# Spreading norm factors as two float32r parts, and state-space products of two heads in turn, in a hybrid decoder layer

## The chip, the cores and the metric

The kernel runs on one core of one Trainium2 chip. The metric is the device time of one execution in microseconds (us); a stated time is the median of several runs. Profiles are of one execution. The engines are named as in the profile: PE is the matrix engine (TensorE), PEld its weight loads, DVE VectorE, ACT ScalarE, POOL GpSimd and SP SyncE, which here only starts transfers.

## What is computed

One layer on 512 tokens of 1024 features, all in float32. Shortened from the reference:

```python
h = x
h = h + 0.5 * swiglu(rmsnorm(h, ffn1_norm), ...)               # D_FF 2816
n = rmsnorm(h, mix_norm)
u, v, z, xbc, dt_raw = split(n @ w_in)                         # 1024, 1024, 1024, 1536, 16
ya = rmsnorm(chunked_spatial_gating(gelu(u), gelu(v)), gm_out_norm)
yb = mamba2_mixer(z, xbc, dt_raw, ...)                         # ends in an rmsnorm in two groups
h = h + concatenate([ya, yb]) @ w_out
h = h + 0.5 * swiglu(rmsnorm(h, ffn2_norm), ...)
gate = sigmoid(rmsnorm(h, ple_norm) @ ple_w_gate + ple_b_gate)
h = h + gate * (p @ ple_w_proj)
return rmsnorm(h, final_norm)
```

An rmsnorm multiplies every token by one factor, rsqrt of the mean of its squared features (plus a small constant), and every feature by a gain. Inside the Mamba-2 mixer (`ssd_chunked`) the 512 tokens are cut into four chunks of 128, and 16 heads of 64 features share two groups of B and C vectors with 128 state features. Per head and chunk, with C·B a 128x128 matrix of the group:

```python
y_diag = ((C B) * decay_of_the_head) @ (x * dt)                # inside the chunk
y_off  = (C @ state_carried_into_the_chunk) * exp(a_cs)        # chunks 1, 2, 3 only
y      = y_diag + y_off + x * d_skip
y      = y * silu(z)                                           # then the rmsnorm of the group
```

## The kernel before, in words

**Layout.** Everything is kept with features on the 128 partitions and the 512 tokens along the free axis, so one tile is 128 features by 512 tokens, and 1024 features are eight tiles. Chunk c of a tile is its columns 128c to 128c+127.

**Large products.** A float32 weight or activation is cut in two float32r numbers, a high part (a copy rounded to float32r) and a low part (the number less its high part). A product is made of three float32r passes, high with high, high with low, low with high (`passes`, lines 199 to 201, called by `accumulate`). The FFNs use the same three passes on sums and differences of tiles (line 617). Weights come by DMA; ACT makes the high part (line 417), DVE the low part (line 421).

**Order of the work.** The whole kernel but its last stage is a list of steps, each a product with its load and split. `run` writes the instruction order of PE, ACT, DVE and SP from that list: the product of a step, the split of the weights for a later step, what was put "after" a step, and what was put on PE behind the product of a step. These engines then execute in exactly that order; only the last stage (per-layer embedding and final norm) is ordered by the scheduler. The mix stage's steps have the order "B0 B1 dt C0 C1 x0 v0 x1 x2 x3 v1 x4 x5 v2 x6 x7 z0 v3 z1 v4 z2 v5 z3 v6 z4 v7 z5 u0 z6 u1 z7 u2 ... u7", each a projection of 128 features (B, C, x, z, u feature-major, v token-major). `first(n, ...)` and `post(n, ...)` put work of DVE, ACT and POOL at step n, ahead of and behind its other work; `on_pe(n, ...)` puts PE work behind the product of step n.

**A norm** (`Norm`, from line 234). Squares are summed over the tiles; PE sums them over the partitions with a column of ones (`sums`), which gives one number per token with tokens on the partitions, 128x4. `of_sums` takes the rsqrt there in small DVE steps (lines 214 to 222). To multiply feature-major tiles, the factor of each token is needed on all 128 partitions. `diagonals` (DVE, line 280) multiplies an identity matrix by the factors, four 128x128 diagonal matrices side by side in one 128x512 tile of the ring "tmp", which has three buffers. `spread` (PE, line 291) multiplies them by a 128x128 matrix of ones in float32: every output row is then the row of factors. `kept` (ACT, line 297) copies that from PSUM to SBUF, the tile "rall". Seven norms go this way: ahead of the first FFN, ahead of the mix stage, the two groups of the Mamba-2 mixer, the spatial gating's output (in the code "gm"), ahead of the second FFN, and ahead of the per-layer embedding.

In the first FFN the first factors meet the gate at line 721 (DVE), after `kept`. DVE writes a tile "embt" (line 528) behind the first diagonal, and ACT copies it to "xfa" (line 530) ahead of `kept`.

**State-space products.** The heads are taken in eight pairs j = 0 to 7; pairs 0 to 3 are of group 0. For a pair, one step of the list after another: ACT turns two tiles of cumulated sums into decays (`decayed`, lines 1313 and 1317); DVE multiplies each head's decays by C·B (`times_cb`, line 1321); PE does `ssd`; DVE and POOL add and gate the result (`gated`, from line 1342); its square is added to the norm of its group. `ssd(j)` stands on PE behind the product of the step after z_j. Its products are float32. For y_diag (line 1331) there are eight: for head 0 and then head 1, for each of the four chunks, one product with 64 columns of x·dt as weights (64 features) and the head's 128x128 decays as moving data. Head 0's results go to partitions 0 to 63 of the PSUM bank `pa`, head 1's to partitions 64 to 127. For y_off (line 1336) there are three, for chunks 1 to 3, each with the carried state of both heads, all 128 features, as weights and the chunk's C as moving data, into the bank `pb`.

Group 0's norm follows pair 3, group 1's pair 7 (`normed_group`): sums on PE behind one product, diagonals on DVE at the next step, spread on PE behind that step's product. The spatial gating's `spatial` takes sums of tiles over partitions with float32r ones (line 1422) from the high and low parts "convin" (ACT line 183, DVE line 184).

In the prediction, "pair 1" to "pair 8" are j = 0 to 7.

## Time and profile before

| quantity | value |
|---|---|
| median of 3 runs | 1097.27 us (1097.17 to 1097.84) |
| span of the profiled execution | 1096.2 us |
| PE matmuls | 1079.8 us, 99% of the span, 6639 instructions |
| PE weight loads | 952.6 us, 87% |
| DVE | 777.0 us, 71%, 1057 instructions |
| ACT | 520.4 us, 47%, 715 instructions |
| POOL | 153.6 us, 14%, 139 instructions |
| moved by DMA | 161.67 MB, on average 147 GB/s |
| line 417, high parts of weights, ACT, 138 of the shape 128x1024 | 144.3 us, 1045 ns each |
| line 421, low parts of weights, DVE, 137 of them | 172.8 us, 1261 ns each |

The span is the time between the first and the last instruction of one core's execution. Times of instructions are counted from its start. A row of the timeline has the start, the duration, the engine, the line of the code, the operation, output<-inputs, their sizes, and x with the number of instructions that the row joins; in brackets stands the time that the engine waited ahead of it and what released it. A float32 product leaves two records of PE, a float32r product one, so that the eight products of line 1331 are "x16". A wait is written as engine, tile and line that waits, an arrow, and the engine, tile and line that released it, then the time in all, the number of waits and the longest. A row of the stretches has begin:end, length, then the busy time and number of instructions of PE, PEld, DVE, ACT and POOL, then the granted clock of PE (1.00 is full), the busy share of DMA, and GB/s; where one line of code is selected, an engine that has none of it is left out.

### The profile page before, as it was taken

How to read it: one execution, taken by the hardware profiler on the slowest of the kernel's cores; microseconds unless marked ns; L12 is line 12 of the kernel's file. 1: busy time of each engine (PE TensorE's matmuls, PEld its weight loads, DVE VectorE, ACT ScalarE, POOL GpSimd, SP SyncE). 2: the span in 40 equal slices, each digit the busy share in tenths (PEclk: the TensorE clock that was granted, in tenths of full speed). 3: DMA queues.
4: the chain of work that ended last, by engine and by line, in shares of the span. 5: the costliest groups of instructions: out<-in, count | busy, mean ns of one | idle time of the engine just before them, and what ended most of it. 6: DMA issues, size and time to landing. Idle time of an engine off the chain costs nothing.

```text
span 1096.2 us, 16449 instructions
## 1 busy us (share of the span) xinstructions
PE 1079.8 (99%) x6639; PEld 952.6 (87%) x6639; DVE 777.0 (71%) x1057; ACT 520.4 (47%) x715; POOL 153.6 (14%) x139
## 2 busy tenths in 40 slices
PE   9999999999999999999999999999999999999997
PEld 7789999999998788787878888889999999999886
DVE  7787776776666696756888566678766776767766
ACT  6554434344444455474673343454444344344554
POOL 3411000000000300133223000000000000000411
PEclk9999999999999999999999999999999999999999
DMA  9758766565623233444333233567766766643412
GB/s 358 202 148 235 193 161 177 168 188 149 177 56 117 80 97 95 135 135 135 101 111 96 77 97 106 176 159 213 198 158 183 193 178 188 163 126 101 147 41 78
DMA packets 49037, 161.67 MB, mean 147 GB/s; under 512 B 5568, under 2 KB 5824, under 8 KB 48960
## 3 DMA queue, kind: packets, MB, share of 16 engines
q1 hardware_dynamic: 38288, 124.80, 33.8%
q0 software_dynamic: 9232, 33.56, 16.9%
q10 hardware_dynamic: 1440, 2.26, 0.6%
q8 instruction: 52, 0.85, 0.3%
q14 instruction: 25, 0.20, 0.1%
HBM read 156.33 MB, written 4.26 MB: 146 GB/s over the span
## 4 chain that ended last, share of the span: by engine, by line
PE 87%; DVE 6%; ACT 3%; issue 2%; DMA 1%; SPq 0%; POOL 0%; DVEq 0%; ACTq 0%; POOLq 0%
PE mm L617 18%; PE a L617 14%; PE sm L200 10%; PE sm L199 10%; PE sm L201 10%; PE mm L200 4%; PE mm L201 4%; PE mm L199 4%; PE a L199 3%; PE a L201 3%; PE a L200 3%; DVE wlo L421 2%; ACT whi L417 1%; DMA h<-in_x 1%; PE sm L1331 1%
## 5 line engine op out<-in xcount | busy, mean ns | idle before, releaser
L417 ACT CAST whi<-raw 128x1024 fp32r<-128x1024 f32 x138 | 144.3, 1045 | 167.2 <-issue 58.9
L421 DVE TENSOR_TENSOR wlo<-raw,whi 128x1024 fp32r<-128x1024 f32 x137 | 172.8, 1261 | 66.5 <-ACT whi L417 62.8
L617 PE MATMUL mm<-xfb,whi 128*128 128x256 f32 x960 | 166.7, 276 | 0.2 <-ACT a L731 0.2
L617 PEld LDWEIGHTS mm<-xfb,whi 128*128 128x128 f32 x960 | 146.2, 188 | 2.0 <-ACT a L731 0.4
L617 PE MATMUL mm<-xfb,wlo 128*128 128x256 f32 x480 | 133.0, 277 | 0.3 <-DVE wlo L421 0.3
L201 PE MATMUL sm<-ghi,wlox 128*128 128x512 f32 x296 | 116.3, 393 | 0.0
L200 PE MATMUL sm<-glo,whix 128*128 128x512 f32 x296 | 115.9, 391 | 0.0
L199 PE MATMUL sm<-ghi,whix 128*128 128x512 f32 x296 | 115.1, 389 | 0.0
L617 PE MATMUL a<-xfb,whi 128*128 128x256 f32 x640 | 111.2, 276 | 1.0 <-DVE g L749 1.0
L617 PEld LDWEIGHTS a<-xfb,whi 128*128 128x128 f32 x640 | 97.9, 188 | 3.2 <-issue 1.6
L617 PEld LDWEIGHTS mm<-xfb,wlo 128*128 128x128 f32 x480 | 90.2, 188 | 0.7 <-DVE wlo L421 0.7
L617 PE MATMUL a<-xfb,wlo 128*128 128x256 f32 x320 | 88.6, 277 | 1.1 <-DVE wlo L421 1.1
L421 DVE TENSOR_TENSOR wlox<-rawd,whix 128x1024 fp32r<-128x1024 f32 (+1 forms) x40 | 45.7, 1142 | 59.0 <-ACT whix L417 59.0
L421 DVE TENSOR_TENSOR wlo<-rawb,whi 128x1024 fp32r<-128x1024 f32 x52 | 64.7, 1246 | 25.1 <-ACT whi L417 24.9
L755 ACT ACTIVATE g<-g 128x512 f32<-128x512 f32 x40 | 25.3, 632 | 108.9 <-DVE g L754 108.9
L632 POOL DMA_DIRECT2D raw<-in_ffn_gu x20 | 17.2, 860 | 390.5 <-DVE h L809 108.1
L809 DVE SCALAR_TENSOR_TENSOR h<-sm,h 128x512 f32<-128x512 f32 x96 | 63.2, 684 | 5.9 <-PE sm L201 5.3
L251 POOL TENSOR_TENSOR ssum<-ssum,tmp 128x512 f32<-128x512 f32 x33 | 50.0, 1514 | 123.3 <-ACT tmp L250 117.6
L417 ACT CAST whi<-rawb 128x1024 fp32r<-128x1024 f32 x52 | 54.1, 1043 | 26.7 <-DVE rawb L627 20.0
L201 PEld LDWEIGHTS sm<-ghi,wlox 128*128 128x128 f32 x296 | 55.5, 188 | 11.6
L199 PEld LDWEIGHTS sm<-ghi,whix 128*128 128x128 f32 x296 | 55.6, 188 | 10.9
L200 PEld LDWEIGHTS sm<-glo,whix 128*128 128x128 f32 x296 | 55.5, 188 | 10.8
(410 smaller groups left out, 2537.0 us busy)
## 6 DMA issues: line engine op xcount, KB each, us to landing
raw<-in_ffn_gu SPq DMA_DIRECT2D x56, 512.0 KB, 5.7
rawd<-in_ffn_down SPq DMA_DIRECT2D x40, 512.0 KB, 4.0
rawb<-in_ffn_gu SPq DMA_DIRECT2D x32, 512.0 KB, 5.3
raw<-in_ffn_gu POOLq DMA_DIRECT2D x30, 512.0 KB, 5.5
raw<-in_w_in SPq DMA_DIRECT2D x29, 512.0 KB, 3.6
s<-in_ffn_gu SPq DMA_DIRECT2D x20, 512.0 KB, 7.0
s<-in_ffn_gu POOLq DMA_DIRECT2D x20, 512.0 KB, 8.3
raw<-in_w_out SPq DMA_DIRECT2D x16, 512.0 KB, 3.5
```

The costliest lines, as they stand in the source:

```text
L199: nc.tensor.matmul(ps, whi, xhi, start=first, stop=False)
L200: nc.tensor.matmul(ps, whi, xlo, start=False, stop=False)
L201: nc.tensor.matmul(ps, wlo, xhi, start=False, stop=last)
L251: self.engines[i].tensor_tensor(self.totals[i], self.totals[i], sq, ALU.add)
L417: nc.scalar.copy(self.hi[:, : self.n], self.raw[:, : self.n])
L421: nc.vector.tensor_tensor(self.lo[:, :n], self.raw[:, :n], self.hi[:, :n].bitcast(F32), ALU.subtract)
L617: nc.tensor.matmul(o, wt[:, c], xt, start=fresh and p == m == n == 0, stop=last and n == 2, skip_group_check=True,)
L632: nc.gpsimd.dma_start(w21.raw, self.src[0], accum_op=ALU.add)
L755: nc.scalar.activation(t, t, AF.Silu)
L809: nc.vector.scalar_tensor_tensor(h[d], ps[d], 0.5, h[d], ALU.mult, ALU.add)
L1331: nc.tensor.matmul(pa[i * HD : (i + 1) * HD, c * P : (c + 1) * P], xdt[g][c][:, k : k + HD], chunk(ms[i], c), start=True, stop=True,)
```

## The change

**Norm factors.** `diagonals` now cuts the 128x4 factors into a high float32r part (a DVE copy) and a low part (a DVE subtraction), in a new ring "tokp" of four small buffers, and makes two diagonal tiles, both in float32r and both from the ring "tmp", which keeps its three buffers. `spread` makes two float32r products with float32r ones, added up in the same PSUM bank. This holds for all seven norms.

**State-space products.** In `ssd`, the chunks are now the outer loop and the two heads the inner one, so that the products of head 0 (partitions 0 to 63) and head 1 (64 to 127) come in turn. The carried state's product of each chunk is cut in two, of 64 features each, into the two halves of `pb`: six products in place of three.

**Address space.** Three paddings shrink by 128 bytes.

The order of everything else is the same: ACT, POOL and SP have the same instructions in the same order, DVE has 21 more (three per norm), and PE has the seven spreads and the 24 products of the carried state twice.

```diff
 BUFS = {
...
-    "nv": 2, "ny": 2, "nt": 2, "bnst": 4, "rlast": 2,
+    "tokp": 4, "nv": 2, "ny": 2, "nt": 2, "bnst": 4, "rlast": 2,
...
-PAD = {"sb": 96, "ffn_left": 384, "mix_left": 448, "ple_left": 448, "ffn_right": 0, ...
+PAD = {"sb": 96, "ffn_left": 256, "mix_left": 320, "ple_left": 320, "ffn_right": 0, ...
...
         def diagonals(tok):
-            diag = tmp()
-            nc.vector.tensor_tensor(
-                diag.rearrange("p (c t) -> p c t", c=NC),
-                ident.unsqueeze(1).to_broadcast([P, NC, P]),
-                tok.unsqueeze(2).to_broadcast([P, NC, P]),
-                ALU.mult,
-            )
-            return diag
+            parts = []
+            hi, lo = (sb("tokp", (P, NC), F32R) for _ in range(2))
+            nc.vector.tensor_copy(hi, tok)
+            nc.vector.tensor_tensor(lo, tok, hi.bitcast(F32), ALU.subtract)
+            for part in (hi, lo):
+                diag = sb("tmp", dt=F32R)
+                nc.vector.tensor_tensor(
+                    diag.rearrange("p (c t) -> p c t", c=NC),
+                    ident.unsqueeze(1).to_broadcast([P, NC, P]),
+                    part.bitcast(F32).unsqueeze(2).to_broadcast([P, NC, P]),
+                    ALU.mult,
+                )
+                parts.append(diag)
+            return parts
 
-        def spread(diag, ps=None):
+        def spread(diags, ps=None):
             ps = sm_ps() if ps is None else ps
-            nc.tensor.matmul(ps, ones, diag, start=True, stop=True)
+            for i, diag in enumerate(diags):
+                nc.tensor.matmul(ps, ones_r, diag, start=i == 0, stop=i == 1)
             return ps
...
         pa, pb = mix["y", j] = ring_ps(), ring_ps()
-        for i in range(2):
-            k = (2 * j + i - 8 * g) * HD
-            for c in range(NC):
+        for c in range(NC):
+            for i in range(2):
+                k = (2 * j + i - 8 * g) * HD
                 nc.tensor.matmul(
                     pa[i * HD : (i + 1) * HD, c * P : (c + 1) * P], xdt[g][c][:, k : k + HD],
                     chunk(ms[i], c), start=True, stop=True,
                 )
         for c in range(1, NC):
-            nc.tensor.matmul(
-                chunk(pb, c), chunk(state[g][c], j - 4 * g), chunk(cT[g], c), start=True, stop=True
-            )
+            for i in range(2):
+                k = (2 * j + i - 8 * g) * HD
+                nc.tensor.matmul(
+                    pb[i * HD : (i + 1) * HD, c * P : (c + 1) * P], state[g][c][:, k : k + HD],
+                    chunk(cT[g], c), start=True, stop=True,
+                )
```

More of the change, by code (lines that the diff above doesn't have):

```diff
@@ L57 @@
 )
-PAD = {"sb": 96, "ffn_left": 384, "mix_left": 448, "ple_left": 448, "ffn_right": 0, "mix_right": 96, "ple_right": 0}
+PAD = {"sb": 96, "ffn_left": 256, "mix_left": 320, "ple_left": 320, "ffn_right": 0, "mix_right": 96, "ple_right": 0}
 HEADS = 16
```

## The prediction

> **What bounds the kernel now.** I read the page first, then the waits of TensorE (PE) over the whole run, then the busy time of two stretches.

> ```profile
> span 1096.2 us, 16449 instructions
> PE 1079.8 (99%) x6639; PEld 952.6 (87%) x6639; DVE 777.0 (71%) x1057; ACT 520.4 (47%) x715; POOL 153.6 (14%) x139
> ```
> ```profile
> PE a L617 <- DVE wlo L421: 1.1, 2, 0.7
> ...
> PE a L617 <- DVE g L749: 1.0, 1, 1.0
> ```
> ```profile
> 529.50:556.00 26.50, 26.09 (x129) 20.96 (x128) 24.96 (x52) 19.76 (x37) 7.25 (x6) 1.00 0.49 144
> ...
> 590.00:716.00 126.00, 126.00 (x575) 104.07 (x574) 82.44 (x129) 49.79 (x68) 6.91 (x6) 1.00 0.37 115
> ```

> PE is busy for 99% of the span, so a microsecond taken off PE is normally a microsecond of time. The waits show the exceptions: in the first FFN PE waits for VectorE (DVE). The stretches (columns: length, then PE, PEld, DVE, ACT, POOL busy, clock) show a second place: from 529.5 to 556.0 us DVE works 24.96 of 26.50 us, almost without a pause, while from 590 to 716 it has 43.6 us to spare. A change that saves PE time and adds DVE time gains at the second kind of place and loses at the first. This change does both, so I sum it by place. The profiled span is 1096.2 us and the median time 1097.27: 1.07 us lie around the span, which I leave as they are.

> **State-space products, one of the eight head pairs.**

> ```profile
> 497.18 0.39 PE L201 MATMUL a<-whi,x 128*128 128x512 f32 x1
> 497.50 1.58 PE L1331 MATMUL a<-u,yb 128*64 128x128 f32 x16
> 499.01 0.94 PE L1336 MATMUL sm<-ya,yb 128*128 128x128 f32 x6
> 499.78 1.02 PE L1267 MATMUL sm<-u,ya 128*128 128x512 f32 x2
> ```
> ```profile
> 497.55:497.98 0.43, 0.43 (x4) 0.43 (x5) 1.00 1.08 414
> 497.98:498.42 0.44, 0.44 (x10) 0.44 (x9) 1.00 0.84 326
> 498.42:498.86 0.44, 0.44 (x9) 0.41 (x4) 1.00 0.55 191
> ```

> Every float32 matmul leaves two records. The second fence has line 1331 alone; its second count is weight loads. With one head running there are 4 to 5 loads in 0.44 us, a step of 0.11 us per record; in the middle, where the end of head one meets the start of head two, 9 in the same time. So two 64-column halves of the array already run side by side for four steps, because the second head's products start before the first head's last ones. Before: 4 steps alone, 4 shared, 4 alone and one long first step, 13 steps, and then 6 of line 1336 at 0.77/6 = 0.13 with their start, 19 steps in all. After, with heads in turn, the 16 records of line 1331 need 8 shared steps and the 12 of the new line 1336 another 6: 14 steps. The two changes between whole and half array stay two. Five steps of 0.11 are 0.55 us; I take **0.50 us per pair**, as the first step after such a change is longer. If nothing ran side by side there would be 28 steps, 1.0 us more than now; that is the other bound.

> [...]

> **Spread.** Seven spreads are float32 products of 512 columns; each becomes two float32r products.

> ```profile
> 376.56 0.69 DVE L280 TENSOR_TENSOR tmp<-ident,rtok 128x512 f32<-128x512 f32 x1
> ...
> 377.92 1.02 PE L291 MATMUL sm<-tmp,ones 128*128 128x512 f32 x2
> ...
> 379.01 0.40 PE L200 MATMUL sm<-x,whi 128*128 128x512 f32 x1
> ```
> ```profile
> 564.71 0.63 PE L1422 MATMUL sm<-convin,onesr 128*128 128x512 f32 x2
> 565.18 0.39 PE L199 MATMUL mm<-x,whi 128*128 128x512 f32 x1
> ```
> ```profile
> 590.50 0.16 DVE L221 SCALAR_TENSOR_TENSOR nt<-nt,nv 128x4 f32<-128x4 f32 x1
> 590.70 0.16 DVE L222 SCALAR_TENSOR_TENSOR rtok<-nt,ny 128x4 f32<-128x4 f32 x1
> 590.90 0.69 DVE L280 TENSOR_TENSOR tmp<-ident,rtok 128x512 f32<-128x512 f32 x1
> 591.51 0.74 DVE L1503 SCALAR_TENSOR_TENSOR tmp<-sm,vec,xs 128x512 f32<-128x512 f32 x1
> ...
> 592.77 0.74 DVE L1503 SCALAR_TENSOR_TENSOR tmp<-sm,vec,xs 128x512 f32<-128x512 f32 x1
> ```
> ```profile
> L280 DVE TENSOR_TENSOR tmp<-ident,rtok x7: 691/692/694, 41.6 to 1045.9; 128x512 f32<-128x512 f32 x7
> ```
> ```profile
> L291 PE MATMUL sm<-tmp,ones x14: 590/591/593, 43.6 to 1048.5; 128*128 128x512 f32 x14
> ```

> Two float32r products with the same ones take 565.18 - 564.71 = 0.47 us. The float32 one takes from 377.92 to the next product's second matmul at 379.01, less that product's first (0.23): 0.86. PE gains **0.40 us** per spread. DVE pays: a copy and a subtraction on 128x4, one small step of 0.20 each (590.50 to 590.70), and a second diagonal, 591.51 - 590.90 = 0.61. That is **1.0 us** more on DVE ahead of everything queued behind it, seven times. Where does it show?

> - *Second norm (mix).* The diagonal ends at 377.25, PE wants it at 377.92. The low one is now there at 378.25 and PE wants it at 378.15: with the signal a wait of 0.15. Gain 0.25.
> - *Second group, gm, ffn2, ple.* Spread and diagonal stand further apart (first 43.6 against 42.3, last two records 1048.1 and 1048.5 against 1046.6). Gain 0.40 each, 1.6 together. In the second group the ring of three tmp buffers adds a wait: the 592.77 instruction now writes the high diagonal's buffer and cannot start before the spread has read it, some 2.4 us later; a weight split and the gating behind it wait too. Cover: the 43.6 us that DVE has free from 590 to 716. Without it up to 2.4 us would be lost.
> - *First norm (ffn1) and first group*: the two places where DVE leads, below.

> **First FFN.**

> ```profile
> ACT xfa L530 <- DVE embt L528: 4.1, 1, 4.1
> ACT ghi L774 <- DVE g L728: 3.0, 1, 3.0
> ```
> ```profile
> DVE g L721 <- ACT rall L297: 1.2, 1, 1.2
> ```

> These waits lie between 41 and 62 us. Behind the first diagonal on DVE stands embt (line 528); ScalarE (ACT) waits 4.1 us for it, and only then, in its own order, copies the spread (rall, line 297), for which DVE waits 1.2 us. So the spread is not what is late; DVE is, and a shorter spread gains nothing here. The chain runs on over the gate and the splits to the waits of PE quoted at the start. All of it moves by 1.0 us: **+1.0**. Bounds: 0, if a pause takes it up, to +1.4, if ACT loses a turn too; the 1.2 us of line 721 is no slack, as rall itself is late by line 530.

> **First group's norm to the spatial sums.**

> ```profile
> 554.31 0.68 DVE L1321 TENSOR_TENSOR u<-u,ya 128x512 f32<-128x512 f32 x1
> 555.53 0.69 DVE L1321 TENSOR_TENSOR u<-u,ya 128x512 f32<-128x512 f32 x1 [0.54 <-ACT u L1317]
> 558.02 0.84 DVE L184 TENSOR_TENSOR convin<-xs,convin 128x512 fp32r<-128x512 f32 x1 [1.80 <-ACT convin L183]
> ```
> ```profile
> ACT yb L183 <- DVE xs L1380: 5.0, 3, 3.3
> ```
> ```profile
> 554.34 0.39 PE L201 MATMUL mm<-x,wlo 128*128 128x512 f32 x1
> 555.14 2.23 PE L1331 MATMUL sm<-u,yb 128*64 128x128 f32 x16 [0.41 <-DVE u L1321]
> ...
> 558.92 0.50 PE L1422 MATMUL sm<-convin,onesr 128*128 128x512 f32 x1 [0.38 <-DVE convin L184]
> ```

> Its chain begins with PE's sums of squares, which come right behind pair 5 of 8, and then DVE is full until 556. ACT hangs on it (5.0 us of waits for line 1380), and the last two waits above hang on ACT. The 1.0 us of DVE reaches the second line 1321 (556.22 to 557.22) and the spatial sums (558.92 to 559.92). What PE saves here, 0.40 by the spread and 0.50 by pair 6, ends in a longer wait in front of pair 7. That pair also changes its kind of wait: its second product needs the second head's decays, so it starts on head one at 556.0, stands until 557.3, and does its 13 remaining steps by 558.9, before the sums can start anyway. Counted from the sums of squares: **+1.0**; bounds 0 and +1.5.

> Pair 8:

> ```profile
> 570.41 0.69 DVE L1321 TENSOR_TENSOR u<-u,ya 128x512 f32<-128x512 f32 x1 [1.14 <-ACT u L1317]
> ```
> ```profile
> 570.74 1.58 PE L1331 MATMUL a<-u,yb 128*64 128x128 f32 x16
> ```

> PE would start at 570.74, but head two's decays end at 571.10. It waits 0.4 of its 0.5: -0.1.

> **Sum.** Pairs 1 to 5: 5 x -0.50 = -2.5. Mix spread -0.25, four more -1.6. First FFN +1.0, first group to sums +1.0, pair 8 -0.1. Together -2.45: 1097.27 - 2.45 = **1094.8**. No other engine's order changes, and no DMA moves past another; the pads are address space alone.

> **Rivals.**

> *The clock falls in the longer wait.*

> ```profile
> 33.30:36.70 3.40, 1.91 (x9) 1.19 (x7) 3.40 (x3) 0.00 (x0) 3.32 (x2) 1.00 1.01 307
> ...
> 1088.00:1091.40 3.40, 0.82 (x7) 0.58 (x7) 2.27 (x8) 1.47 (x3) 0.00 (x0) 1.00 0.30 110
> 1091.40:1096.20 4.80, 0.00 (x0) 0.00 (x0) 0.00 (x0) 0.00 (x0) 0.00 (x0) 0.50 0.59 220
> ```

> After 3.4 us with PE busy for 0.82 the granted clock fell to 0.50; 1.91 of 3.4 did not do it. By the forecast PE would be done at 553.7, do 0.25 us of pair 7 and stand until 557.3: a tenth of 3.6 us. If that cuts the clock for about as long, the 1.5 us of pair 7 take 3.0 and the sums slip; since PE was to wait for the sums anyway, 0 to 1.2 us are lost. I take 0.8: **1095.6**. Against it: whether such a stretch is counted as one depends on where it begins. [...]

> *DVE's microsecond is taken up* at both places by pauses that I count as full. PE still gains nothing there, since it waited there before: -2.5 - 1.85 - 0.1, **1092.8**.

> *The halves do not pair* (the slower side). Place: lines 1331 and 1336; price +1.0 per pair. Five pairs +5.0; pair 7 would end late enough to make +1.0 into +1.8; pair 8 +1.3; with the first FFN and the spreads 5.0 + 1.8 + 1.3 + 1.0 - 1.85 = +7.2: **1104.5**. It decides once about a quarter of the steps stay alone. Against it: the nine loads.

> That the change does not do what it says comes to this same rival.

> **How the numbers follow.** Forecast 0.45, clock 0.30, taken up 0.12, no pairing 0.06, unnamed 0.07 split evenly. A measurement of this kernel tells about 0.2% (2.2 us) from no change, so 1095.1 divides faster from same. Of the forecast I put 0.30 below that line and 0.15 above; of the clock case 0.06 and 0.24; taken up counts as faster, no pairing as slower. Faster 0.50, same 0.42, slower 0.08. The range 1093.4 to 1096.6 holds forecast and clock with the bounds of their terms, and leaves most of the other two out. Faster and same are both gains here; the forecast alone has 1094.0 to 1095.6.

> **What would show it.** Right: line 1331 to the next whole-array matmul 1.8 us in place of 2.3 in pairs 1 to 5; a pause of PE of over 2 us in front of pair 7 where 0.41 stood, and PE's idle time in the first FFN up by 1.4; spreads of 0.47. The clock case shows a granted clock under 1.00 near 557. Wrong: weight loads at one step each in line 1331, no longer pause at pair 7, or a new wait of PE between 590 and 640 for a weight split.

## The result and the profile after

The changed kernel takes 1093.84 us (median of 6 runs, 1093.19 to 1094.19), against 1097.25 us before (6 runs): a ratio of 0.9966, 95% interval 0.9955 to 0.9978. That is 3.4 us less; 2.45 were forecast, 1094.8 us, and the range was 1093.4 to 1096.6. In a second set of 6 runs the changed kernel took 1094.01 us against 1097.25 us.

The page of the changed kernel begins so:

```profile
span 1092.5 us, 16566 instructions
PE 1073.4 (98%) x6687; PEld 949.0 (87%) x6687; DVE 781.8 (72%) x1078; ACT 520.2 (48%) x715; POOL 153.4 (14%) x139
```

PE is busy for 6.4 us less, DVE for 4.8 us more, and the span is 3.7 us shorter, so PE also stands still for 2.7 us more. (Every run's time is 1.7 us above its span, not 1.07 as the prediction took it; the profiled execution of before, with its span of 1096.2 us, took longer than the median one, whose span is 1095.5.) The lines of code behind `diagonals` have moved by 7, those behind `ssd` by 10: L1331 is now L1338, L1336 is L1345, L1422 is L1432. The two waits of PE that grew most (time in all, number, longest):

```profile
PE sm L1338 <- DVE u L1328: 2.6, 2, 1.9
...
PE mm L624 <- ACT a L738: 1.6, 1, 1.6
```

The second is in the first FFN, where 0.2 us stood before (ACT line 731): the 1.4 us more that were forecast. The first is the pause ahead of pair 7, 2.6 us in place of 0.41. What follows the pause, again of the changed kernel, first the timeline of PE, then busy time and clock (the third number from the end) in three stretches:

```profile
553.24 0.40 PE L1338 MATMUL sm<-u,yb 128*64 128x128 f32 x2 [1.87 <-DVE u L1328]
554.39 1.02 PE L1338 MATMUL sm<-u,yb 128*64 128x128 f32 x13 [0.75 <-DVE u L1328]
...
555.22 1.69 PE L1345 MATMUL a<-ya,yb 128*64 128x128 f32 x11
556.83 1.22 PE L1432 MATMUL sm<-convin,onesr 128*128 128x512 f32 x2
557.85 0.63 PE L199 MATMUL sm<-x,whi 128*128 128x512 f32 x1
```
```profile
552.50:555.00 2.50, 1.01 (x14) 0.80 (x16) 1.28 (x2) 2.47 (x6) 0.00 (x0) 1.00 0.50 201
555.00:558.50 3.50, 3.50 (x24) 2.89 (x21) 2.36 (x5) 2.83 (x6) 1.27 (x1) 0.53 0.00 0
558.50:562.00 3.50, 3.50 (x16) 2.85 (x16) 3.50 (x6) 1.13 (x1) 0.25 (x1) 0.98 0.24 51
```

The granted clock was 0.53 on average from 555.0 to 558.5 us (in the trace, 0.50 from 555.20 to 558.61): the first rival came true. A pass of line 199 then takes 0.63 us, where 0.39 is the usual.

A pair of heads in the changed kernel (pair 3, the same as in the prediction):

```profile
496.26 0.39 PE L201 MATMUL a<-whi,x 128*128 128x512 f32 x1
496.58 1.09 PE L1338 MATMUL a<-u,yb 128*64 128x128 f32 x16
497.50 0.82 PE L1345 MATMUL sm<-ya,yb 128*64 128x128 f32 x12
498.26 1.12 PE L1274 MATMUL sm<-u,ya 128*128 128x512 f32 x2
```

From the last projection pass to the next whole-array product stand 2.00 us, where 497.18 to 499.78, 2.60, stood. From line 1338 (1331 before) it is 1.68 in place of 2.28; 1.8 in place of 2.3 was forecast. The 28 records run two at a time. Of the 0.60 gained, 0.10 is paid back at once, as the first product behind the change to the whole array takes 1.12 in place of 1.02.

To see where the time went, I matched PE's instructions of each run with those of before and read how much earlier (-) or later (+) each starts. The table has the difference over five places: the first FFN (from the sums of squares of the first norm to before's 70 us), pairs 1 to 5 (465 to 529.4), the first group (529.4 to 560.2, which holds its spread, pair 6, pair 7 and the spatial sums), pair 8 (569 to 574), and the later spreads (574 to 1050 less 0.26, which before's own profile loses between 720 and 780 us against all kernels but one). "Clock" says whether it fell near 556 us in the profiled execution.

| kernel | first FFN | pairs 1-5 | first group | pair 8 | later spreads | clock |
|---|---|---|---|---|---|---|
| forecast | +1.0 | -2.5 | +1.0 | -0.1 | -1.6 | stays |
| changed | +0.81 | -2.57 | +1.40 | -0.50 | -1.69 | falls |
| changed, again | +0.82 | -2.56 | +1.38 | -0.51 | -1.70 | falls |
| e1, spread alone | +0.79 | 0 | +0.71 | 0 | -1.73 | stays |
| e2, heads alone | 0 | -2.56 | +1.17 | -0.50 | 0 | falls |
| e3, two norms whole | 0 | -2.56 | +0.31 | -0.11 | -1.74 | stays |
| e4, pause filled | +0.80 | -2.56 | +0.57 | -0.11 | -1.70 | stays |
| e5, only the first products in turn | 0 | -2.44 | +0.29 | -0.10 | 0 | stays |
| e8, DVE's work added | +1.06 | 0 | +0.91 | 0 | 0 | stays |
| e9, pair 7 in order | 0 | -2.56 | +0.28 | -0.08 | -1.75 | stays |
| e11, changed, pair 7 in order | +0.96 | -2.57 | +0.57 | -0.10 | -1.70 | stays |

In the profiled executions of e1, e4, e5, e6, e8, e10 and of the changed kernel's second set the clock also falls to half for 3.4 us near 38 us. Where the first norm is as before (e5, e6, e10), the first FFN loses nothing by it (0.0 in all three). In e7 and e11 it lasts 6.8 us; e11's 0.96 in place of 0.81 may be its work.

The mix norm's spread lies between the places of the first two columns: -0.32 in the changed kernel, -0.25 forecast.

### The profile page after: what moved, and what is told of

It is laid out like the page before. It is cut to its first block, busy times and chain, and to the rows that moved or that the text cites. A ratio compares the mean times of both kernels' runs of the same rounds, so it can differ in the third digit from the quotient of the medians.

```text
span 1092.5 us, 16566 instructions
## 1 busy us (share of the span) xinstructions
PE 1073.4 (98%) x6687; PEld 949.0 (87%) x6687; DVE 781.8 (72%) x1078; ACT 520.2 (48%) x715; POOL 153.4 (14%) x139
## 4 chain that ended last, share of the span: by engine, by line
PE 86%; DVE 7%; ACT 4%; issue 2%; DMA 1%; SPq 0%; POOL 0%; DVEq 0%; ACTq 0%; POOLq 0%
PE mm L624 19%; PE a L624 14%; PE sm L200 10%; PE sm L199 10%; PE sm L201 10%; PE mm L200 4%; PE mm L199 4%; PE mm L201 4%; PE a L199 3%; PE a L201 3%; PE a L200 3%; DVE wlo L428 2%; ACT whi L424 1%; DVE tmp L1620 1%; DMA h<-in_x 1%
## 5 line engine op out<-in xcount | busy, mean ns | idle before, releaser
L201 PE MATMUL sm<-ghi,wlox 128*128 128x512 f32 x296 | 116.3, 393 | 0.0
L200 PE MATMUL sm<-glo,whix 128*128 128x512 f32 x296 | 115.8, 391 | 0.0
L199 PE MATMUL sm<-ghi,whix 128*128 128x512 f32 x296 | 115.1, 389 | 0.0
L201 PEld LDWEIGHTS sm<-ghi,wlox 128*128 128x128 f32 x296 | 55.5, 188 | 11.7
L200 PEld LDWEIGHTS sm<-glo,whix 128*128 128x128 f32 x296 | 55.5, 188 | 10.9
L199 PEld LDWEIGHTS sm<-ghi,whix 128*128 128x128 f32 x296 | 55.6, 188 | 10.8 <-DVE h L816 0.2
```

The source lines that it names most:

```text
L199: nc.tensor.matmul(ps, whi, xhi, start=first, stop=False)
L200: nc.tensor.matmul(ps, whi, xlo, start=False, stop=False)
L201: nc.tensor.matmul(ps, wlo, xhi, start=False, stop=last)
```

## The experiments

The theory: PE's saving counts wherever PE leads; at two places DVE leads, and there its added work is added to the time. The rivals: DVE's work costs nothing, or the loss ahead of pair 7 is the clock's.

**e1, the spread alone.** Edit: `ssd` as before.

> The spread part of the change alone (state-space products as before). Theory (sum by place): PE's saving counts where PE leads, DVE's extra microsecond where DVE leads. First FFN +0.9, mix spread -0.28, first group to the spatial sums +0.7, four later spreads -1.8 together: -0.5, 1096.7 us; clock 1.00 throughout; the wait of PE ahead of line 624 for ACT line 738 is 1.6 us as in the changed kernel. Rival A (DVE's extra work costs nothing): six or seven spreads of -0.4, 1094.6 us. Rival B (the clock falls even without the heads in turn, as the pause before pair 7 is made by DVE alone): granted clock 0.5 near 556 us and 1097.5 us.

Measured: 1096.18 us (11 runs), ratio 0.9993, interval 0.9984 to 1.0002, against 1097.04. The medians differ by 0.9 us, and the interval reaches no change. By place the theory holds: +0.79 and +0.71 where DVE leads, -1.73 at the four later spreads. These two losses rule out rival A, and rival B falls as the clock near 556 us stays at 1.00. One expected sign didn't come: the wait for ACT line 738 is not among PE's. PE's clock was 0.76 on average from 36 to 43 us in this execution, so PE came later by itself, and the first FFN still lost the same 0.8.

**e2, the heads alone.** Edit: `diagonals` and `spread` as before.

> The state-space part of the change alone (spread in float32 as before). Theory: pairs 1 to 5 gain 0.52 each, pairs 6 and 7 nothing as DVE sets the time of the spatial sums, pair 8 gains 0.5: -3.1, 1094.2 us; first FFN unchanged; PE's pause ahead of pair 7 is about 0.9 us and the clock stays 1.00. Rival (the clock falls here too, since pair 7 now also waits for its second head's decays): granted clock 0.5 near 556 us and 1095.0 us.

Measured: 1095.24 us (11 runs, 1094.68 to 1097.07), ratio 0.9983, interval 0.9974 to 0.9992. The rival was right: the clock falls here too.

```profile
552.50:555.00 2.50, 0.79 (x10) 0.58 (x12) 1.52 (x3) 2.47 (x6) 0.63 (x1) 1.00 0.61 243
555.00:558.50 3.50, 3.50 (x27) 2.98 (x24) 2.14 (x5) 2.62 (x5) 1.27 (x1) 0.53 0.00 0
```

So DVE's added work isn't needed for it. With heads in turn pair 7 waits twice, once for each head's decays (1.9 us together), and the clock can fall then. It need not: e5 waits twice as well, 1.9 us together, and keeps 1.00. Nor does it fall in every run of e2: two of the 11, of 1094.70 and 1094.72 us, have a mean clock of 0.998, and no profiled execution with a fall on the way has more than 0.997. The profiled execution, of 1096.42 us, also lost 1.2 us between 70 and 300 us, outside the table's places. The change gains more than e1 and e2 together (0.9 and 1.8), since their losses overlap: in the first group e1 loses 0.71 and e2 1.17, the change 1.40 and not 1.88.

**e3, two norms whole.** The places where DVE leads keep one float32 diagonal. Edit:

```diff
-        def diagonals(tok):
+        def diagonals(tok, whole=False):
             parts = []
+            if whole:
+                diag = tmp()
...
+                return [diag]
...
-                diags = self.diagonals(self.of_sums(got["ps"], n))
+                diags = self.diagonals(self.of_sums(got["ps"], n), whole)
...
-        norm.diagonals(norm.of_sums(mix["g", g], D // GROUPS))
+        norm.diagonals(norm.of_sums(mix["g", g], D // GROUPS), g == 0)
```

`whole` is true for "ffn1", and `spread` makes one float32 product of a single diagonal.

> The changed kernel, but the first FFN's norm and the first group's norm keep the one float32 diagonal and product. Theory: pairs 1 to 5 -2.6, mix spread -0.28, four later spreads -1.8, pair 8 -0.5: -5.2, 1092.1 us, the clock stays 1.00 at pair 7, and PE's wait ahead of line 624 of the changed kernel (ACT line 738) is back at 0.2 us. Rival A (the loss in the first FFN was made up later, so nothing is won back there): 1093.0 us. Rival B (the clock falls all the same): 1093.0 us with a granted clock of 0.5 near 556 us.

Measured: 1092.38 us (5 runs, 1092.19 to 1094.05), ratio 0.9959, interval 0.9947 to 0.9972, 1.5 us below the changed kernel and 0.3 above the theory. The wait of PE that the theory named, in the lines of this kernel (0.2 us before):

```profile
PE mm L636 <- ACT a L750: 0.4, 1, 0.4
```

The loss of the first FFN is gone, 0.8 us. The first group still loses 0.31 though DVE has no more to do there: pair 6's gain isn't passed on, and a part of pair 5's is lost. My reading, which no run tests: ACT's chain to the decays of pairs 6 and 7 begins behind a projection pass that comes ahead of pair 5, so that pair 5's gain doesn't reach it. The row of before:

```profile
526.40 1.04 ACT L417 CAST whi<-raw 128x1024 fp32r<-128x1024 f32 x1 [3.56 <-PE a L201]
```

**e4, the pause filled.** Edit, in `ssd` ahead of the products; their results are overwritten:

```diff
+        if j == 6:
+            for _ in range(8):
+                nc.tensor.matmul(pa, ones_r, x[0][0], start=True, stop=True)
```

> The changed kernel with eight added float32r products of 512 columns ahead of pair 7, whose results are overwritten: 1.8 us of work for PE in a pause of 2.25 us. Theory (half the loss around pair 7 is the clock): granted clock 1.00 throughout, 0.9 us less than the changed kernel, 1092.9 us. Rival A (the loss is DVE's lateness, the clock only fills a wait): no difference, 1093.8 us. Rival B (the added work delays pair 7): up to 1.8 us more, 1095.6 us.

Measured: 1093.51 us (5 runs, 1093.32 to 1093.59). The clock stays:

```profile
552.50:555.00 2.50, 1.72 (x22) 1.13 (x22) 1.04 (x2) 2.47 (x5) 0.17 (x1) 1.00 0.35 142
555.00:558.50 3.50, 3.09 (x23) 2.23 (x20) 2.69 (x6) 3.44 (x5) 1.11 (x1) 1.00 0.00 0
```

1.8 us of added work made the kernel no slower; its median is 0.3 to 0.5 us below those of the changed one, not the 0.9 expected, and too near to be told from none by the times alone. The table says why: the first group loses 0.57 in place of 1.40, so the fall costs 0.83 there; but pair 8 then gains 0.11 in place of 0.50. With the fall PE comes to pair 8 at 569.73, when head two's decays have been there since 569.21; in e4 it comes at 568.56, and they are there at 568.89. 0.4 of the 0.8 comes back 10 us later.

**e5 and e6, one half of the state-space part each.** e5 takes heads in turn in line 1331 alone; e6 splits the carried state's products alone. Both are parts of the change's diff.

> The kernel before with the heads in turn in the products inside the chunk alone; the carried state's products stay whole (128 features, three per pair), the spread stays float32. Theory (pairing of column halves, and 0.2 us for each change between half and whole array): the first products take 0.92 us in place of 1.51, then a change of 0.2 in place of 0.1, then the state's 0.77: 2.09 us from the last projection pass to the next product in place of 2.60, and 2.00 with both. Time about 0.5 us above the state-space part alone, 1095.7 us. Rival (the split of the state's products is worth its share of steps, half of the gain): 2.30 us per pair, 1096.3 us.

> The kernel before with the carried state's products in two halves of 64 features alone; head one's four products first, then head two's, as before. Theory: head one's half array goes on to its six records of the state's products while head two still runs alone, so that 2.40 us stand in place of 2.60 per pair: about -1.1 us, 1096.0 us. Rival (a half starts the state's products only when both heads are done): 2.59 us per pair, no difference, 1097.0 us.

Measured: e5 1095.14 us (10 runs), ratio 0.9980, interval 0.9971 to 0.9989; e6 1097.25 us (10 runs), ratio 1.0002, interval 0.9993 to 1.0011. Pair 3 of e5, then of e6:

```profile
495.96 0.39 PE L201 MATMUL a<-whi,x 128*128 128x512 f32 x1
496.27 1.09 PE L1331 MATMUL a<-u,yb 128*64 128x128 f32 x16
497.30 0.94 PE L1336 MATMUL sm<-ya,yb 128*128 128x128 f32 x6
498.07 1.02 PE L1267 MATMUL sm<-u,ya 128*128 128x512 f32 x2
```
```profile
496.39 0.39 PE L201 MATMUL a<-whi,x 128*128 128x512 f32 x1
496.71 1.25 PE L1331 MATMUL a<-u,yb 128*64 128x128 f32 x13
497.70 0.32 PE L1338 MATMUL sm<-ya,yb 128*64 128x128 f32 x1
...
498.88 1.13 PE L1267 MATMUL sm<-u,ya 128*128 128x512 f32 x2
```

e5 has 2.11 us per pair, as its theory had it, and pays nothing behind it (1.02). Its time did not follow the theory: I had expected 0.5 us more than e2, and it is the same. By the table e5 gains 0.12 less in the pairs, and its profiled execution is spared the fall of the clock that e2's has. e6 has 2.49, and 1.13 behind: no gain, and its theory (1.1 us less) fell. Head one's half does go ahead (line 1338 starts while line 1331 has 3 records to come), but the same stretch ends no sooner than six whole products would. So the change's gain per pair comes from the turns in line 1331; splitting the state's products moves 0.1 us from the middle of a pair to its end.

**e7, two chunks of a head at a time.** Edit: in e2, the order of line 1331 is chunks 0 and 1 of head one, the same of head two, then 2 and 3 of each.

> The state-space part alone with another order: two chunks of head one, the same two of head two, then the other two of each. Theory (each half of the columns takes its own products in turn, some ahead of the program's order): no different from strict turns, 2.00 us per pair from the last projection pass to the next product. Rival (only direct neighbours of unlike halves run side by side): 12 or 13 steps alone or shared in place of 8, 2.4 us per pair.

Measured: 2.05 us per pair, 2.00 in strict turns. The theory holds: neighbours in the program needn't alternate. (Its one run took 1097.4 us, with a clock of 0.56 from 36 to 43 us and a wait of 0.7 us for a weight split near 105 us; the first is in runs of other kernels too, the second in that of e2. I draw nothing from that time.)

**e8, DVE's work alone.** Edit: before, with the copy, the subtraction and the second diagonal added behind the first, which nobody reads.

> The kernel before with the change's DVE instructions added (copy, subtraction and second diagonal, whose result nobody reads), the spread in float32 as before. Theory: 0.8 us each in the first FFN and from the first group's sums to the spatial sums, nothing elsewhere: +1.5 us, 1098.5 us. Rival A (taken up by pauses): 1097.0 us. Rival B (DVE leads at more places, as the ring of three tmp buffers turns twice as fast): 1099.5 us or more, with waits of PE for line 421 or 1354 behind the second group's norm.

Measured: 1099.33 us (10 runs), ratio 1.0018, interval 1.0009 to 1.0027: +2.2 us, 0.7 more than the theory. In the profiled execution it is lost at the two places named, +1.06 and +0.91, and at no other of the table's; a third place, as rival B has it, isn't there. The size is that of DVE's rows, of e8 and then of the changed kernel, at the first norm:

```profile
40.58 0.16 DVE L222 SCALAR_TENSOR_TENSOR rtok<-nt,ny 128x4 f32<-128x4 f32 x1
40.84 0.69 DVE L280 TENSOR_TENSOR tmp<-ident,rtok 128x512 f32<-128x512 f32 x1
41.45 0.16 DVE L287 CAST tokp<-rtok 128x4 fp32r<-128x4 f32 x1
...
42.52 1.22 DVE L430 TENSOR_TENSOR wlo<-raw,whi 128x1024 fp32r<-128x1024 f32 x1
```
```profile
40.97 0.16 DVE L222 SCALAR_TENSOR_TENSOR rtok<-nt,ny 128x4 f32<-128x4 f32 x1
41.17 0.17 DVE L281 CAST tokp<-rtok 128x4 fp32r<-128x4 f32 x1
41.37 0.16 DVE L282 TENSOR_TENSOR tokp<-rtok,tokp 128x4 fp32r<-128x4 f32 x1
41.45 1.29 DVE L285 TENSOR_TENSOR tmp<-ident,tokp 128x512 fp32r<-128x512 f32 x2
42.66 1.22 DVE L428 TENSOR_TENSOR wlo<-raw,whi 128x1024 fp32r<-128x1024 f32 x1
```

The added rows of e8 take 41.45 to 42.52, 1.07 us; those of the changed kernel 1.69 less the 0.87 from 40.58 to 41.45, 0.82 us. The first FFN loses 1.06 in e8 and 0.81 in the changed kernel: there, DVE's time is the kernel's time, one for one.

**e9, e10, e11, pair 7 in order.** e9 is e3, and pair 7 takes head one's products first. e10 is e9 with the state's products whole. e11 is the changed kernel with e9's edit:

```diff
-        for c in range(NC):
-            for i in range(2):
+        order = [(c, i) for c in range(NC) for i in range(2)]
+        if j == 6:
+            order.sort(key=lambda ci: ci[1])
+        for c, i in order:
```

> As e3_two_norms_whole (float32 spread at the first FFN's and the first group's norm), and pair 7 takes its heads one after the other in the products inside the chunk, so that PE works on head one while it waits for head two's decays. Theory: the spatial sums start no earlier, since DVE line 184 sets them, but PE stands still for less, so the clock stays 1.00 in every run: 1092.2 us, the least seen in runs of e3_two_norms_whole, with a smaller spread. Rival (the second wait did cost): 0.4 us less, 1091.9 us or below.

> As e9_pair7_in_order, but the carried state's products stay whole (three per pair). Theory (splitting them is worth nothing by itself): 1092.4 us as e9_pair7_in_order, to within 0.3 us. Rival (the change from half to whole array at the end of a pair costs more than in the middle): 0.5 us more, 1092.9 us.

> The changed kernel, but pair 7 takes head one's products first, so that PE works while it waits for head two's decays. Theory (the clock's fall costs what e4_filled won back): clock 1.00 near 556 us and 1093.4 us. Rival A (the clock falls all the same, as the first wait of 1.9 us suffices): 1093.8 us. Rival B (taking the heads in order costs its 0.5 us here): 1094.2 us.

> The changed kernel once more, beside the two that follow. 1093.8 us; granted clock 0.5 near 556 us, mean clock 0.996 or less in every run.

Measured: e9 1092.39 us (5 runs, 1092.24 to 1093.60), ratio 0.9959, interval 0.9945 to 0.9972; e10 1092.42 us (5 runs, 1092.24 to 1092.62), 0.9954, interval 0.9942 to 0.9967; e11 1093.81 us (5 runs, 1093.44 to 1094.43); the changed kernel again 1094.01 us (6 runs, 1093.37 to 1094.83). e9 equals e3, so the second wait of pair 7 cost nothing there, and e10 equals e9, so the split of the state's products is worth nothing. In e11 the clock near 556 us stays at 1.00 and the first group loses 0.57 as in e4, but its time is 0.4 us above its theory and only 0.2 us below the changed kernel's: the direction of e4, too little to be told from none by the times alone. In the changed kernel's second set one run of six has a mean clock of 0.997, where 0.996 or less was expected of all; whether the clock fell near 556 us in that run isn't known. e3, e9 and e10 are alike and the best versions tried, 1.5 us below the changed kernel.

## Why the prediction was right, and where it wasn't

The sign and the range held: 0.34% faster, interval 0.22% to 0.45%. By its steps:

*Pairs 1 to 5:* right in size, -2.57 for -2.5, and in cause. The count has all five steps in line 1331 (13 to 8) and none in the state's products (6 to 6). e5 shows 0.49 (2.60 to 2.11) in line 1331 alone, and in e6 the split of the state's products alone gains nothing. That the halves pair is in the rows of the changed kernel: 28 records in 2.00 us, two to a step of 0.11.

*Spreads:* -0.32 in the mix stage for -0.25, and -1.69 for -1.6 behind. DVE's cover from 590 to 716 us held: no wait of PE for a weight split appeared, and the second group gained its 0.4.

*First FFN:* right in cause and place; the wait of PE rose by 1.4 us as forecast. The size was +0.81 for +1.0. The mis-sized term is DVE's: the two small steps and the second diagonal take 0.82, not 1.0, since the first diagonal starts 0.08 us behind the subtraction, where I had counted 0.20. It doesn't read the subtraction's result. In these rows such an instruction starts 0.08 us ahead of the end of the one before (41.45 against 41.53, in the changed kernel and at the copy of e8), and one that reads it starts behind that end.

*First group:* the step that failed, though the time came out in the range. I wrote that PE's pause ahead of pair 7 leaves the clock alone and DVE's microsecond costs 1.0. The pause fell as forecast (2.6 us, "over 2 us"), but the clock went to 0.53, as the first rival had it. Without the fall the place costs 0.57 (e4, e11), and with it 1.40: the rival's 0.8 in addition was right. What it left out is the next place, pair 8, which gave 0.4 back. Part of the 0.57 isn't DVE's microsecond either: without any DVE work added the place loses 0.3 (e3, e5), since the gains of pair 6 and of part of pair 5 don't get through.

*Pair 8:* -0.1 is right where the clock stays, -0.50 where it falls.

So the case that came true is the rival "the clock falls", with chance 0.30, and its time of 1095.6 was still 1.8 us too high. Its sum in rows: -2.57 - 0.32 + 0.81 + 1.40 - 0.50 - 1.69 = -2.87. The end of the kernel adds -0.3: from the last product to the end of the span stand 7.38 us in every kernel with the two-part spread in the last norm, 7.68 in the others. I had no such term, and what makes it stays open. Together that is -3.2, against -3.2 and -3.4 in the two sets of runs. Of the rival's -1.65, the first group was 0.4 too slow (1.0 and 0.8 for 1.40), pair 8 0.4, the first FFN 0.2, pairs and spreads 0.2 together, and the end, 0.3, was missing.

That the forecast of 1094.8, which has the clock wrong, came nearer (1.0 us) than the rival that has it right is luck: its first group was 0.4 too cheap and its pair 8 gained 0.4 too little, and the two cancel.

*The slower side:* the halves pair, so 1104.5 us never came near. *DVE's microsecond taken up:* shown wrong by e8.

That the fall has to do with the pause is shown by e4: with the pause filled, the clock stays; the 0.72 and 0.39 us of waiting that are left there keep PE busy for two thirds of any 3.4 us. The length of the pause alone doesn't settle it, since e2 and e3 both wait 1.9 us and only e2's clock falls. The traces show what differs. In the changed kernel the fall lasts 3.413 us (555.201 to 558.614). In each of the traces the first rise of the clock and its last fall are a whole number of 3.413 us apart (316 to 318 of them), and the changes between lie on the same grid. I counted how long PE was busy in the stretches of that grid near 556 us, in all 14 profiled executions. In the stretch that ends where the clock falls it was busy for 0.35 of the time (changed kernel), 0.27 (its second set) and 0.44 (e2). In the eleven without a fall the least busy stretch has 0.54 or more. e2's two waits lie in one stretch; those of e3 are divided between two. First the stretch of e2, with 1.49 us of PE in 3.41, then the two of e3:

```profile
551.78:555.19 3.41, 1.49 (x15) 0.86 (x15) 2.21 (x5) 3.38 (x8) 0.63 (x1) 1.00 0.62 201
```
```profile
548.75:552.16 3.41, 1.85 (x9) 1.19 (x7) 3.03 (x11) 3.37 (x8) 0.63 (x1) 1.00 0.80 241
552.16:555.58 3.42, 2.66 (x30) 1.89 (x30) 1.61 (x3) 3.42 (x5) 1.28 (x1) 1.00 0.10 40
```

The pause of e11, 1.9 us, is divided too (0.82 and 0.60 busy). That its clock stayed may then be owed to where its grid lay, and isn't proof that the shorter wait prevents the fall. The prediction's own doubt, that it depends on where the stretch begins, was well founded. A border between 0.44 and 0.54 doesn't hold everywhere: near 37 us the clock fell behind a stretch with PE busy for 0.71 (changed kernel, second set) and stayed behind one with 0.57 (before). What counts there stays open.

## What to carry to other kernels

A saving on the busiest engine is worth its time only where that engine leads. Before a change that pays with another engine is put everywhere, look for the stretches in which that other engine never rests, and leave the old form there: two of seven norms cost this change 1.5 us of a possible 4.8. And price a pause of PE with what follows it: of the 0.8 us that the fallen clock cost, the next wait gave 0.4 back.

## What the runs showed of the hardware

In these runs products of 64 columns whose results go to unlike halves of the partitions ran side by side, two to a step of 0.11 us (in the changed kernel 10 weight loads of line 1338 in 0.45 us, where one head alone had 4 to 5 in 0.44), even where the program has two of a head before two of the other (e7: 2.05 us per pair, 2.00 in strict turns). The change from halves back to the whole array cost about 0.1 us in the kernel before: line 1336 starts 0.20 us behind the last half-array record (498.81 to 499.01), where 0.11 is the step of these records.
